# Second output projection opened five tiles wide, the last four differential heads spaced by four slots, their masks added by VectorE

## The chip, the cores and the metric

The kernel runs on one core of a Trainium2 chip. The metric is the device time of one execution in microseconds (us); a lower time is better. A time is given as the median of several runs, and one further execution is profiled; all rows of a trace come from that one.

## The reference

A two-layer decoder trunk on 256 tokens of width 2048, batch 1, in float32. Layer 0 mixes by causal pooling and a cross-attention to a memory of 256 rows; then a squared-ReLU MLP. A shared key and value projection follows. Layer 1, where the change lies, computes

```python
a = probs(q1b, k1) - lam * probs(q2b, k2)      # 12 heads, two softmax maps of width 64
o = einsum('bhqk,bkhd->bqhd', a, v)            # per head 128 wide; causal mask inside probs
token_out = rms_norm(o, subln_norm[b]) * (1.0 - lam_init)
mem_out = memory_cross_attention(...)          # 4 heads of 128, no mask
x = x + concat([token_out, mem_out]) @ w_out[1]
x = x + squared_relu_mlp(rms_norm(x, ffn_norm[1]), w_ff1[1], w_ff2[1])
```

Inside `probs` every score whose key lies behind its query gets -1e30 before the softmax. The queries stand in two blocks of 128: the first block sees 128 keys, the second 256, and in each the last 128 columns of the scores carry the triangular mask.

## The kernel before, in words

**Layout.** Activations lie transposed: 16 chunks of 128 channels by 256 tokens. Each weight is split into a high part (fp32r, a rounded float) and a low rest; a product takes the high weight against the activation's high and low halves (512 columns) and the low weight against the high half (256 columns). A block is one 128x128 weight; a group of four blocks is one 128x512 tile, loaded by SyncE, copied to the high ring by ScalarE (L158) and subtracted to the low ring by VectorE (L159). The rings have six places (`SLOTS`), and a group is prepared three groups ahead of its use (`AHEAD`).

**Slots.** `tick()` runs once each time four blocks have been used. `at(d, fn)` puts a function d slots ahead; so attention work is strewn between the matmuls of a projection. A slot in `c_tile` (L415 to L417) is four blocks with three matmuls of 256 columns each, a slot in `a_part` (L401, L403) four blocks with one matmul of 512 and one of 256 columns. The tile framework then orders each engine's instructions; engines work through their queues in that order.

**A differential head** (`diff_head`): `scores` multiplies queries and keys into two banks of tag "s" (of two), adds the mask, and has VectorE take the maxima (L1219) and ScalarE the exponentials (L1223). With `by_pe` the mask is added by TensorE, as an extra bf16 product of an identity with the mask into the same bank (L1200 to L1205: four pairs of a product and a mask product); otherwise VectorE adds it in place (L1209, L1212 the products, L1214 and L1215 the additions). Four slots later `turn` transposes the probabilities (L1238). At `pv_lag` slots, `pv` multiplies them with the values into the one bank of tag "o" (L1244 to L1246); ScalarE squares and sums (L1254), the reciprocal root follows, and VectorE scales into `osb` (L1262). With `by_pe` the bank is copied to `osb` first (L1249). `back_lag` slots on, `back` transposes the result (L1267) into its chunk of `cat1`.

**The heads' places.** The 12 heads come in three groups c of four. Heads of c = 0 and 1 start at slots 6, 10, 14, 18 after their query projection, without `by_pe`. Those of c = 2 start at 6, 8, 10, 12 with `by_pe`, their PV six slots on, their way back three more. Meanwhile four `c_tile` calls (four slots each) make the memory queries, and each memory head (`mem_head`) follows with scores (L583, one bank of "s") 4 slots after its tile, the transposition (L602) 8 and PV (L610, the bank "o") 11 after; its result is copied and subtracted into `cat1` chunks 12 to 15 (L611, L612).

**The second output projection** (`out_tiles`, call at the end of layer 1's attention). 16 output tiles, each the sum over 16 chunks of `cat1`. Three banks of tag "mm" serve the tiles. Tiles 0 to 2 are opened with a `lead` of 15 chunks in three parts, then `flush` empties the slots, then each of the three gets its last chunk `ks` = [15], and tiles 3 to 15 follow whole. A finished tile is added to the residual by two VectorE additions (L648, L649), which free its bank; then `resid_done` makes the next stage's input. The same function serves layer 0 with one lead of 13 chunks.

The MLP after it (`ffn`) takes over all banks; its first slab preparation is held back in the order until tile 2's addition (`feed.gate`).

Of the kernel before, what the change touches and what calls it, by code (L numbers as in the profile page):

```python
# [10 lines left out]
F32 = mybir.dt.float32  # L11
# [7 lines left out]
P = 128  # L19
T = 256  # L20
NK = 16
# [34 lines left out]
class Plan:  # L56
# [13 lines left out]
    def close(self):  # L70
        prep = []
        for job in self.jobs:

            late = job[0] == "S" and job[1] % 32 > 28
            if job[0] == "S" and job[2] == 0 and not late:
                prep.insert(max(0, len(prep) - KOFF), ("K", job[1]))
            if late and job[2] == 1:
                prep.append(("L", job[1]))
            prep.append(job)
        self.prep = prep  # L80
        self.where = {job: i for i, job in enumerate(prep)}
        self.loads = []
        self.need = {}
        for p in prep:
            if p[0] == "K":
                self.loads += [("S", p[1], 0), ("S", p[1], 1)]
            elif p[0] == "L":
                self.loads.append(("S", p[1], 1))
            elif p[0] == "S" and p[2] == 0 and ("S", p[1], 0) not in self.loads:
                self.loads.append(("S", p[1], 0))  # L90
            elif p[0] == "N" and p[1] % 2 == 0:
                self.loads.append(("N", p[1] // 2))
            self.need[p] = len(self.loads) - 1
        rows = sorted(self.loads, key=lambda r: r[0] == "N" and 8 * r[1] + 8 > self.npos)
        self.row = {r: h for h, r in enumerate(rows)}
        of = {}
        pos = 0
        for what in self.entries:
            of.setdefault(pos // 8, []).append(what)
            pos += what[4]  # L100
        self.order = []
        for r in rows:
            self.order += of[r[1]] if r[0] == "N" else self.slabs[r[1]][r[2]]
# [169 lines left out]
def program(ctx, tc, plan, dry, xT, memT, par, lam, cst, wst, yT):  # L273
# [5 lines left out]
    pp = ctx.enter_context(tc.tile_pool(name="pp", bufs=1, space=PSUM))  # L279
# [10 lines left out]
    def at(d, fn):  # L290
        pend.setdefault(now[0] + d, []).append(fn)

    def tick():
        now[0] += 1
        for fn in pend.pop(now[0], []):
            fn()
# [9 lines left out]
    def mmt(name):  # L306
        return pp.tile([P, 512], F32, tag="mm", bufs=3, name=name)
# [42 lines left out]
    def gcol(c):  # L350
        return param[:, c : c + 1]
# [26 lines left out]
    def split_gain(dst, src, g):  # L378
        nc.scalar.activation(dst[:, 0:T], src, AF.Copy, scale=g)
        stt(dst[:, T : 2 * T], src, g, dst[:, 0:T].bitcast(F32), ALU.mult, ALU.subtract)  # L380
# [6 lines left out]
    def a_part(ps, w, l, n, ks, xs, first=True, last=True, between=None):  # L387


        ks = list(ks)  # L390
        i = 0
        while i < len(ks):
            if between:
                between(i)
            two = []
            for k in ks[i : i + 2 - feed.pos % 2]:
                two.append((i, k % NK, *feed.block((w, l, k, n, 1))))
                feed.used()
                i += 1
            for c, k, hi, lo in two:  # L400
                nc.tensor.matmul(ps, hi, xs[:, k, :], start=first and c == 0, stop=False)  # L401
            for c, k, hi, lo in two:
                nc.tensor.matmul(  # L403
                    ps[:, T : 2 * T], lo, xs[:, k, 0:T], start=False,
                    stop=last and c == len(ks) - 1,
                )
            if feed.pos % 4 == 0:
                tick()
# [215 lines left out]
    def add_square(key, src, first, act=False):  # L624

        if first:
            acc[key] = tp.tile([P, T], F32, tag="acc", bufs=1, name="acc")
            nc.gpsimd.tensor_mul(acc[key], src, src)
            return
        sq = vt("psq")  # L630
        if act:
            nc.scalar.activation(sq, src, AF.Square)
        else:
            nc.gpsimd.tensor_mul(sq, src, src)
        nc.gpsimd.tensor_add(acc[key], acc[key], sq)
# [11 lines left out]
    def resid_add(ps, n):  # L647
        nc.vector.tensor_add(resid[:, n, :], resid[:, n, :], ps[:, 0:T])  # L648
        return nc.vector.tensor_add(resid[:, n, :], resid[:, n, :], ps[:, T : 2 * T])  # L649

    def resid_done(n, splits, square=True):
        for dst, g in splits:
            split_gain(dst[:, n, :], resid[:, n, :], gcol(g + n))
        if square:
            add_square("x", resid[:, n, :], n == 0)
# [295 lines left out]
    cat = sp.tile([P, NK, 512], F32R, tag="S0", name="cat0")  # L951
# [16 lines left out]
    ps = [mmt("mq0"), pp.tile([P, 512], F32, tag="o", bufs=1, name="mq0")]  # L968
# [14 lines left out]
    for h in range(4):  # L983
        mem_head(
            mq0[:, h, :], y0.rearrange("p (t h) -> p t h", t=2)[:, :, h], mk[:, h, :],
            lambda mb, h=h: mv[:, mb, h * P : h * P + P], ebuf[h % 2], pTb, cat[:, 12 + h, :],
# [4 lines left out]
    def group_u(g):  # L991
        up = ups[g % 2]
        for c in range(3):
            ps = mmt("u")
            a_part(ps, "w_in", 0, 3 * g + c, range(NK), xs)
            low = vt("u_c")
            nc.scalar.copy(low, ps[:, T : 2 * T])
            nc.vector.tensor_add(low, ps[:, 0:T], low)
            nc.vector.tensor_mul(up[:, c, 16:], low, x_r[0])
        w = WIN[g]  # L1000
        steps = []
        cur = up
        for i in range(g + 1):
            d = 1 << i
            lo = 2 * d - 1
            nxt = sbs[i % 2]
            steps.append((nxt[:, :, lo:], cur[:, :, lo:], cur[:, :, lo - d : 272 - d]))
            cur = nxt
        for i, (o, a, b) in enumerate(steps):
            at(i + 1, lambda o=o, a=a, b=b: nc.vector.tensor_add(o, a, b))  # L1010
        res = sbs[(g + 1) % 2][:, :, 16:]

        def mean():
            stt(res, cur[:, :, 16:], 1.0 / w, up[:, :, 16:], ALU.mult, ALU.subtract)
            inv = const[:, C_INV : C_INV + w].unsqueeze(1).to_broadcast([P, 3, w])
            nc.vector.tensor_mul(res[:, :, 0:w], cur[:, :, 16 : 16 + w], inv)
            nc.vector.tensor_sub(res[:, :, 0:w], res[:, :, 0:w], up[:, :, 16 : 16 + w])

        at(g + 2, mean)
        for c in range(3):  # L1020
            at(g + 3 + c, lambda c=c: split_plain(pooled[:, 3 * g + c, :], res[:, c, :]))
# [13 lines left out]
                    tick()  # L1035
            split_gain(cat[:, 3 * g + n, :], ps[:, 0:T], gcol(G_PS + 3 * g + n))

    def out_tiles(l, cat, lead, ks, fx, between):

        first = [mmt("wo") for _ in range(3)]  # L1040
        for i, part in enumerate(lead):
            for n in range(3):
                a_part(first[n], "w_out", l, n, part, cat, first=i == 0, last=False)
        between()
        for n in range(NK):
            if n < 3:
                ps = first[n]
                a_part(ps, "w_out", l, n, ks, cat, first=False)
            else:
                ps = mmt("wo")  # L1050
                a_part(ps, "w_out", l, n, sum(lead, []) + ks, cat)
            done = resid_add(ps, n)
            if n == 2 and not dry:
                feed.gate = done.ins.name
            resid_done(n, [(fx, G_FFN + 16 * l)])

    group_u(3)
    group_u(2)
# [9 lines left out]

    fx = sp.tile([P, NK, 512], F32R, tag="S2", name="fx0")
    lead0 = [9, 10, 11, 6, 7, 8, 3, 4, 5, 12, 13, 14, 15]  # L1070
    out_tiles(0, cat, [lead0], [0, 1, 2], fx, last_group)

    x_in = []
    down = ffn(0, fx, ("S1", "S0"), lambda n: resid_done(n, [(x_in[0], G_KV)], False))
# [40 lines left out]
    for c in range(3):  # L1115
        ps = pair_of_banks(c, "k1")
# [10 lines left out]
    for c in range(3):  # L1127
        ps = pair_of_banks(c + 1, "v1")
# [9 lines left out]
    ps = pair_of_banks(0, "mk1")  # L1138
# [4 lines left out]
    ps = pair_of_banks(1, "mv1")  # L1143
# [41 lines left out]
    cat1 = sp.tile([P, NK, 512], F32R, tag="S1", name="cat1")  # L1185
# [90 lines left out]
    for c in range(3):  # L1276
        ps = pair_of_banks(0, "q1")
        b_tile(ps, "w_in_q", 1, c, x_mx)
        rows, v = query_rows(ps, c1, 64)
        rope(rows, qtab)  # L1280
        y = query_scale(v, c1)
        for i in range(2):
            j = 2 * c + i
            q = qb[j % 3]
            at(4 + i, lambda i=i, q=q, rows=rows: turn_queries(rows, 2 * i, q))
            for g in range(2):
                h = 2 * i + g

                diff_head(
                    2 * j + g, q[g], y, *((6 + 4 * h, 8, 4 if c == 0 else 3) if c < 2 else (6 + 2 * h, 6, 3)), c == 2  # L1290
                )
    for h in range(4):
        ps = mmt("mq1")
        c_tile(ps, "w_in", 1, 12 + h, range(NK), x_mx)
        q, y = mem_query(ps[:, 0:T], mqg1, c1)
# [4 lines left out]

    fx1 = sp.tile([P, NK, 512], F32R, tag="S0", name="fx1")

    out_tiles(1, cat1, [list(range(8)), [12, 8, 9, 13], [10, 11, 14]], [15], fx1, flush)

    down = ffn(1, fx1, ("S2", "S1"), lambda n: nc.sync.dma_start(yT[:, n, :], resid[:, n, :]))
    down()
# [83 lines left out]
```

## Time and profile before

| | |
|---|---|
| median of 3 runs | 2046.35 us (2045.26 to 2046.72) |
| time of the profiled execution | 2045.64 us |
| span of its trace | 2043.9 us |
| TensorE busy (matmul) | 2037.5 us, 11060 instructions |
| VectorE busy | 1714.7 us |
| ScalarE busy | 1348.3 us |
| granted TensorE clock | 1.000 |

The span runs from the first to the last instruction; the execution's own time has 1.7 us around it. A row of the timeline gives the start in us from the span's start, the duration in us, the engine, the source line, the operation and the tiles (out<-in), the shape, and how many instructions were merged. Matmuls are pipelined, so a row's duration reaches over the starts of the next ones: what a matmul costs the engine is the distance from its start to the next start. A float32 product counts as two matmuls.

### The profile page before, as it was taken

To read this page: it belongs to the slowest core of one execution; us is meant where nothing else is said; L and a number is where in the kernel's file an instruction comes from. 1 tells how busy PE (TensorE), PEld (TensorE's weight loads), DVE (VectorE), ACT (ScalarE), POOL (GpSimd) and SP (SyncE) were. 2 spreads that over 40 slices of the span, in tenths; PEclk is the share of its full clock that TensorE was granted. 3 is DMA by queue.
4 is the path that set the end of the run, shared out by engine and by line. 5 is a ranking of instruction groups with operands and counts; after the bars stand their busy time and mean duration, and the time that the engine had idled before them with its cause. 6 is when DMAs were issued, how large, how long until landed. Compare 5 with 4: busy or idle time off the path is not lost.

```text
span 2043.9 us, 32256 instructions
## 1 busy us (share of the span) xinstructions
PE 2037.5 (100%) x11060; PEld 1753.8 (86%) x11060; DVE 1714.7 (84%) x3215; ACT 1348.3 (66%) x2505; POOL 52.4 (3%) x67
## 2 busy tenths in 40 slices
PE   9999999999999999999999999999999999999999
PEld 8888888888888888888888888888888888888888
DVE  8788889889879978999765687889879978988997
ACT  7765566667656756768665697566657666666764
POOL 0001200000000000000000000310000000000000
PEclk9999999999999999999999999999999999999999
DMA  8556556556556555655665543556555555565563
GB/s 309 180 180 193 188 171 207 198 186 208 186 197 204 187 205 191 211 169 182 192 228 189 168 141 113 187 166 207 196 195 202 189 196 196 186 207 198 195 209 134
DMA packets 110469, 390.74 MB, mean 191 GB/s; under 512 B 12256, under 2 KB 14944, under 8 KB 110304
## 3 DMA queue, kind: packets, MB, share of 16 engines
q1 hardware_dynamic: 110160, 388.59, 56.9%
q8 instruction: 86, 1.41, 0.3%
q14 instruction: 79, 0.65, 0.1%
q10 hardware_dynamic: 144, 0.10, 0.0%
HBM read 386.54 MB, written 2.10 MB: 190 GB/s over the span
## 4 chain that ended last, share of the span: by engine, by line
PE 99%; ACT 1%; DMA 0%; DVE 0%; SPq 0%; issue 0%
PE x_bank L401 33%; PE x_bank L403 16%; PE wo L401 6%; PE p L756 5%; PE p L757 5%; PE p L758 5%; PE wo L403 3%; PE u L401 2%; PE ff L401 2%; PE u L403 1%; PE k L427 1%; PE k L429 1%; PE v L427 1%; PE k L428 1%; PE v L429 1%; PE v L428 1%
## 5 line engine op out<-in xcount | busy, mean ns | idle before, releaser
L158 ACT CAST hi_ring<-raw 128x512 fp32r<-128x512 f32 x1193 | 736.2, 620 | 522.5 <-PE x_bank L401 300.2
L159 DVE TENSOR_TENSOR lo_ring<-raw,hi_ring 128x512 fp32r<-128x512 f32 x1193 | 815.9, 693 | 200.8 <-ACT hi_ring L158 157.3
L401 PE MATMUL x_bank<-fx,hi_ring 128*128 128x512 f32 x1920 | 601.8, 395 | 0.0
L403 PEld LDWEIGHTS x_bank<-fx,lo_ring 128*128 128x128 f32 x1920 | 360.6, 188 | 84.0
L403 PE MATMUL x_bank<-fx,lo_ring 128*128 128x256 f32 x1920 | 377.2, 278 | 0.0
L401 PEld LDWEIGHTS x_bank<-fx,hi_ring 128*128 128x128 f32 x1920 | 301.2, 189 | 9.4
L401 PE MATMUL x_bank<-z,hi_ring 128*128 128x512 f32 x960 | 301.0, 395 | 0.0
L159 DVE TENSOR_TENSOR lo_ring<-slab,hi_ring 128x1024 fp32r<-128x1024 f32 x188 | 229.9, 1223 | 54.2 <-ACT hi_ring L158 53.4
L158 ACT CAST hi_ring<-slab 128x1024 fp32r<-128x1024 f32 x188 | 196.8, 1047 | 72.9 <-PE x_bank L401 37.5
L403 PEld LDWEIGHTS x_bank<-z,lo_ring 128*128 128x128 f32 x960 | 180.3, 188 | 41.9
L403 PE MATMUL x_bank<-z,lo_ring 128*128 128x256 f32 x960 | 188.6, 278 | 0.0
L401 PE MATMUL wo<-cat,hi_ring 128*128 128x512 f32 x512 | 163.2, 399 | 1.4 <-DVE resid L649 0.8
L401 PEld LDWEIGHTS x_bank<-z,hi_ring 128*128 128x128 f32 x960 | 151.8, 189 | 6.5 <-ACT room L682 0.4
L403 PEld LDWEIGHTS wo<-cat,lo_ring 128*128 128x128 f32 x512 | 95.9, 188 | 21.9
L682 ACT COPY room<-x_bank 128x512 f32<-128x512 f32 x180 | 104.8, 582 | 2.0 <-PE x_bank L403 2.0
L403 PE MATMUL wo<-cat,lo_ring 128*128 128x256 f32 x512 | 101.5, 278 | 0.0
L756 PE MATMUL p<-hi_ring,sit 128*128 128x512 f32 x256 | 100.4, 392 | 0.0
L757 PE MATMUL p<-hi_ring,sit 128*128 128x512 f32 x256 | 100.1, 391 | 0.0
L758 PE MATMUL p<-lo_ring,sit 128*128 128x512 f32 x256 | 99.6, 389 | 0.0
L727 ACT ACTIVATE room<-room 128x256 f32<-128x256 f32 x128 | 53.2, 416 | 45.5 <-DVE room L310 45.3
L401 PEld LDWEIGHTS wo<-cat,hi_ring 128*128 128x128 f32 x512 | 78.8, 189 | 3.1 <-PE wo L403 1.3
L756 PE MATMUL p<-hi_ring,z 128*128 128x512 f32 x192 | 75.1, 391 | 0.0
(313 smaller groups left out, 3099.0 us busy)
## 6 DMA issues: line engine op xcount, KB each, us to landing
raw<-in_w SPq DMA_DIRECT2D x595, 512.0 KB, 3.8
slab<-in_w SPq DMA_DIRECT2D x124, 512.0 KB, 3.5
resid<-in_x SPq DMA_DIRECT2D x8, 256.0 KB, 5.3
room<-in_w SPq DMA_DIRECT2D x4, 512.0 KB, 4.2
memraw<-in_mem SPq DMA_DIRECT2D x4, 512.0 KB, 4.1
out_y<-resid SPq DMA_DIRECT2D x16, 128.0 KB, 1.8
memraw<-in_mem SPq DMA_DIRECT2D x7, 256.0 KB, 6.4
raw<-in_w SPq DMA_DIRECT2D x3, 256.0 KB, 3.7
```

What stands on the lines that cost most here:

```text
L158: self.nc.scalar.copy(hi, src)
L159: self.nc.vector.tensor_sub(lo, src, hi.bitcast(F32))
L401: nc.tensor.matmul(ps, hi, xs[:, k, :], start=first and c == 0, stop=False)
L403: nc.tensor.matmul(ps[:, T : 2 * T], lo, xs[:, k, 0:T], start=False, stop=last and c == len(ks) - 1,)
L427: nc.tensor.matmul(ps[t], xl, hi, start=k == 0, stop=False)
L428: nc.tensor.matmul(ps[t], xh, hi, start=False, stop=False)
L429: nc.tensor.matmul(ps[t], xh, lo, start=False, stop=k == NK - 1)
L682: nc.scalar.copy(x, ps)
L727: at(3, lambda: nc.scalar.activation(stage[i % 8], y[:, 0:T], AF.Square))
L756: nc.tensor.matmul(ps, a[1], hi, start=first, stop=False)
L757: nc.tensor.matmul(ps, a[0], hi, start=False, stop=False)
L758: nc.tensor.matmul(ps, a[0], lo, start=False, stop=last)
```

## The change

Three parts, all in layer 1. First, the last four heads start at slots 6, 10, 14, 18 instead of 6, 8, 10, 12, with PV seven slots on instead of six, and without `by_pe`: VectorE adds their masks, and the copy of the bank "o" (L1249) goes for them, so that the bank is read until the scaling. Second, `out_tiles` opens five tiles: 0 to 2 with 11 chunks in two parts, then 3 and 4 with the same 11 chunks, these two in banks of tag "s"; after the flush each of the five gets the last five chunks 9, 14, 10, 15, 11, and tiles 5 to 15 follow whole in the three "mm" banks. Third, the additions to the residual (`close`) of tiles 1 to 4 are put 1, 3, 7 and 10 slots later. Layer 0 keeps its order.

```diff
-    def out_tiles(l, cat, lead, ks, fx, between):
-        first = [mmt("wo") for _ in range(3)]
-        for i, part in enumerate(lead):
-            for n in range(3):
-                a_part(first[n], "w_out", l, n, part, cat, first=i == 0, last=False)
-        between()
-        for n in range(NK):
-            if n < 3:
-                ps = first[n]
-                a_part(ps, "w_out", l, n, ks, cat, first=False)
-            else:
-                ps = mmt("wo")
-                a_part(ps, "w_out", l, n, sum(lead, []) + ks, cat)
+    def out_tiles(l, cat, lead, ks, fx, between, later):
+        def tile_bank(n):
+            if n in (3, 4):
+                return pp.tile([P, 512], F32, tag="s", bufs=2, name="wo")
+            return mmt("wo")
+
+        def close(ps, n):
             done = resid_add(ps, n)
             if n == 2 and not dry:
                 feed.gate = done.ins.name
             resid_done(n, [(fx, G_FFN + 16 * l)])
+
+        first = []
+        for tiles, parts in lead:
+            for part in parts:
+                for n in tiles:
+                    if n == len(first):
+                        first.append(tile_bank(n))
+                    a_part(
+                        first[n], "w_out", l, n, part, cat, first=part is parts[0], last=False
+                    )
+        between()
+        every = sum(lead[0][1], [])
+        for n in range(NK):
+            if n < len(first):
+                ps = first[n]
+                a_part(ps, "w_out", l, n, ks, cat, first=False)
+            else:
+                ps = tile_bank(n)
+                a_part(ps, "w_out", l, n, every + ks, cat)
+            if n < len(later) and later[n]:
+                at(later[n], lambda ps=ps, n=n: close(ps, n))
+            else:
+                close(ps, n)
...
-    out_tiles(0, cat, [lead0], [0, 1, 2], fx, last_group)
+    out_tiles(0, cat, [(range(3), [lead0])], [0, 1, 2], fx, last_group, ())
...
-                    2 * j + g, q[g], y, *((6 + 4 * h, 8, 4 if c == 0 else 3) if c < 2 else (6 + 2 * h, 6, 3)), c == 2
+                    2 * j + g, q[g], y, 6 + 4 * h, *((8, 4 if c == 0 else 3) if c < 2 else (7, 3)), False
...
-    out_tiles(1, cat1, [list(range(8)), [12, 8, 9, 13], [10, 11, 14]], [15], fx1, flush)
+    parts = [list(range(8)), [12, 8, 13]]
+    lead1 = [(range(3), parts), (range(3, 5), [parts[0] + parts[1]])]
+    out_tiles(1, cat1, lead1, [9, 14, 10, 15, 11], fx1, flush, (0, 1, 3, 7, 10))
```

## Prediction

> **What bounds the kernel now.** I read the page first, then the sums by stretches, TensorE's waits, and the timeline around the change. On the page I look at the engines' shares and at the chain that ended last.
>
> ```profile
> PE 2037.5 (100%) x11060; PEld 1753.8 (86%) x11060; DVE 1714.7 (84%) x3215; ACT 1348.3 (66%) x2505; POOL 52.4 (3%) x67
> PE 99%; ACT 1%; DMA 0%; DVE 0%; SPq 0%; issue 0%
> ```
>
> TensorE works the whole span and is 99% of the chain. So a change gains only what it takes out of TensorE's queue or out of TensorE's idle time. The sums by stretches (busy us and count for each engine) show how little idle time there is where the change lies:
>
> ```profile
> 1200.00:1250.00 50.00, 49.95 (x375) 46.56 (x374) 42.34 (x154) 43.76 (x145) 0.00 (x0) 1.00 0.40 127
> 1250.00:1280.00 30.00, 28.84 (x172) 24.68 (x172) 22.66 (x71) 19.88 (x57) 2.07 (x3) 1.00 0.42 141
> ```
>
> The last four heads start at 1220 and the first output tiles close at 1275. TensorE (first busy column) lacks 0.05 us in the first stretch and 1.16 us in the second. TensorE's waits from 1250 to 1400 name all of the latter:
>
> ```profile
> PE wo L401 <- DVE resid L649: 0.6, 1, 0.6
> PE wo L401 <- DVE cat L612: 0.6, 1, 0.6
> ```
>
> These are the two things that can go: the mask products and two waits at the closing of tiles 0 to 3.
>
> **Part 1: the masks.** One head with masks by TensorE, then one with masks by VectorE, each from its first product to the next projection matmul:
>
> ```profile
> 1225.75 0.60 PE L1200 MATMUL s<-big,att 128*128 128x256 f32 x2
> 1226.18 0.22 PE L1201 MATMUL s<-mkb,idb 128*128 128x128 bf16 x1
> 1226.24 0.65 PE L1200 MATMUL s<-big,att 128*128 128x256 f32 x2
> ...
> 1227.39 0.22 PE L1205 MATMUL s<-mkb,idb 128*128 128x128 bf16 x1
> 1227.42 0.36 PE L415 MATMUL mq<-x_mx,hi_ring 128*128 128x256 f32 x1
> 1227.62 0.28 PE L416 MATMUL mq<-x_mx,hi_ring 128*128 128x256 f32 x1
> 1227.74 0.28 PE L417 MATMUL mq<-x_mx,lo_ring 128*128 128x256 f32 x1
> ```
> ```profile
> 1211.03 1.03 PE L1209 MATMUL s<-big,att 128*128 128x256 f32 x4
> 1211.90 0.61 PE L1212 MATMUL s<-big,att 128*128 128x128 f32 x4
> 1212.26 0.36 PE L415 MATMUL mq<-x_mx,hi_ring 128*128 128x256 f32 x1
> ```
>
> From start to start the first takes 1227.42 - 1225.75 = 1.67 us, the second 1212.26 - 1211.03 = 1.23 us. The difference is 0.44 us a head, four heads: **-1.76 us**. It holds more than the 16 mask matmuls themselves: the distance from the first mask to the next product is 0.06 us, and the product behind it is longer too (0.65 against 0.60). The Trainium skill (TensorE: Matmul & The Clock Gate, section "Wait — 56ns, not 53.3ns?") gives 55.6 ns from start to start for warm bf16 matmuls of 128 columns. The 0.06 us agrees; by that figure alone 16 masks would give an estimate of -0.89 us and the sum would end 0.87 us higher, but the page's figure leaves out what the neighbours lose, and the row decides.
>
> What VectorE takes on, from the groups by shape between 1200 and 1280:
>
> ```profile
> L1214 DVE TENSOR_TENSOR s<-s,const 128x256 f32<-128x256 f32 x2 | 0.9, 428 | 0.2 <-PE s L1209 0.2
> L1249 DVE COPY osb<-do 128x256 f32<-128x256 f32 x4 | 1.7, 420 | 0.3
> L1262 DVE TENSOR_SCALAR osb<-do,o_y 128x128 f32<-128x128 f32 x8 | 2.4, 344 | 0.1
> L1262 DVE TENSOR_SCALAR osb<-osb,o_y 128x128 f32<-128x128 f32 x8 | 1.9, 282 | 0.0
> ```
>
> Eight additions of 0.43 us, less four copies of 0.42, and eight scalings out of the bank at 0.344 instead of 0.282: 3.4 - 1.7 + 0.5 = +2.2 us. VectorE is idle for 7.66 us in the first stretch above and for 7.34 in the second, and its low-ring work is three groups ahead of TensorE. I cost it at nothing; without that cover it is +2.2 us. Behind a mask addition, which waits for the scores, stand ring subtractions on the same queue; those already stand so behind the heads of c = 1, whose additions waited 0.2 us (the row's last number) without a TensorE wait.
>
> **Part 2: the spacing.** Four heads over 12 slots instead of 6 add no instruction. In the built order TensorE leaves the projection for attention work 31 times from just ahead of the first memory-query tile to the end of the output projection, against 29 before; inside the output projection it is 14 against 11. Each return costs a longer first pair. A pair after an interruption, and a quiet one:
>
> ```profile
> 1261.92 0.82 PE L401 MATMUL wo<-cat,hi_ring 128*128 128x512 f32 x2
> 1262.58 0.40 PE L403 MATMUL wo<-cat,lo_ring 128*128 128x256 f32 x2
> ...
> 1278.60 0.62 PE L401 MATMUL wo<-cat,hi_ring 128*128 128x512 f32 x2
> 1279.06 0.40 PE L403 MATMUL wo<-cat,lo_ring 128*128 128x256 f32 x2
> ```
>
> The two high products take 0.66 us against 0.46: 0.20 us. In the memory tile above it is 1227.62 - 1227.42 = 0.20 against 0.12: 0.08 us. Three more of one and one fewer of the other: at most 0.6 - 0.08 = 0.5, at least three of 0.08 less one: 0.16. I take **+0.3 us**, between them.
>
> **Part 3: the closing.** The two waits with their surroundings:
>
> ```profile
> 1275.06 0.28 PE L403 MATMUL wo<-cat,lo_ring 128*128 128x256 f32 x1
> 1275.91 0.50 PE L401 MATMUL wo<-cat,hi_ring 128*128 128x512 f32 x1 [0.57 <-DVE cat L612]
> 1276.25 0.28 PE L403 MATMUL wo<-cat,lo_ring 128*128 128x256 f32 x1
> 1276.36 0.40 PE L401 MATMUL wo<-cat,hi_ring 128*128 128x512 f32 x1
> ...
> 1276.96 0.28 PE L403 MATMUL wo<-cat,lo_ring 128*128 128x256 f32 x1
> 1277.83 0.71 PE L401 MATMUL wo<-cat,hi_ring 128*128 128x512 f32 x2 [0.59 <-DVE resid L649]
> 1278.37 0.39 PE L403 MATMUL wo<-cat,lo_ring 128*128 128x256 f32 x2
> ```
>
> A 256-column matmul costs 0.11 to 0.12 (1276.25 to 1276.36). Here the next start comes 0.85 and 0.87 us later: 0.73 + 0.75. The first products after the gaps cost 0.34 instead of 0.23 and 0.54 instead of 0.46: 0.1 and 0.08. Together **-1.66 us** if both waits go.
>
> They do by count. In the built order, 48 of the 55 opening blocks stand before the last memory PV is done, so 7 blocks and the chunks 9, 14, 10 of tile 0 stand between it and chunk 15: 10 blocks of 0.35 us (0.70 us a pair from 1278.60) are 3.5 us, against 0.73 us that are missing now. Tile 5 needs tile 0's bank only 20 blocks (7 us) after tile 0's last product, against 0.75 us missing now. What would be late next is the last head's chunk 11, the fifth to be closed: its transposition follows the last PV directly, 11 blocks, 3.8 us ahead. The later additions of tiles 1 to 4 lie beside tiles 5 to 15 (11 x 16 blocks of 0.35, 61 us). The memory stays as it is: one slab load stands two places later in SyncE's queue, and the preparation that `feed.gate` holds back moves on with tile 2. I cost these at nothing.
>
> **A new wait.** Without the copy the bank "o" is held until the scaling. Its hold, from the start of PV to the end of the scaling or of the copy, is in three heads (the first two without, the third with the copy):
>
> ```profile
> 1201.67 0.38 PE L1244 MATMUL do<-big,att 128*128 128x128 f32 x2
> 1205.59 0.60 DVE L1262 TENSOR_SCALAR osb<-do,o_y 128x128 f32<-128x128 f32 x2
> ```
> ```profile
> 1230.57 0.39 PE L1244 MATMUL do<-big,att 128*128 128x128 f32 x2
> 1237.83 0.61 DVE L1262 TENSOR_SCALAR osb<-do,o_y 128x128 f32<-128x128 f32 x2
> ```
> ```profile
> 1238.52 0.47 PE L1244 MATMUL do<-big,att 128*128 128x128 f32 x2
> 1239.47 0.42 DVE L1249 COPY osb<-do 128x256 f32<-128x256 f32 x1
> ```
>
> That is 4.5, 7.9 and 1.4 us. The next user of the bank is a memory PV. In the built order TensorE has about 8.6, 8.8, 7.3 and 3.6 us of its own work between the two for the four heads (the last: a PV of 0.7 and 8.3 projection blocks of 0.35). Only the last is short: a hold of 4.5 us stalls it by 0.9, one of 7.9 by 4.3 and the third by 0.6 more. VectorE does mask and maximum work inside the 4.5 us, and the last head has no head behind it, so the hold should be nearer to 4. I take **+0.5 us**, bounds 0 and 4.9. TensorE stands in order, so all projection blocks wait behind that PV.
>
> **Sum.** -1.76 + 0.3 - 1.66 + 0.5 = -2.62 us. The profiled execution took 2045.64 us (1.7 around its span), so its counterpart would take 2043.0; the median is 0.7 higher, 2046.35, and I forecast the median: **2043.7 us**, by -0.13%.
>
> **Rivals.**
> - *The bank "o" is held long (slower).* Price 4.9 instead of 0.5: 2048.1 us. It beats the gain from a last hold of 3.6 + 2.6 + 0.5 = 6.7 us on. For it: the 7.9 us row, in a heavily loaded stretch. Against it: few other heads are left then. The Trainium skill (PSUM — Partial Sum Buffer, section "Summary: rules for kernel authors") says to evacuate promptly, which speaks against dropping the copy. By that rule this rival holds; the 1.4 us row agrees that the copy frees the bank early. Chance 0.13.
> - *VectorE becomes the bound.* All of its +2.2 us falls on TensorE: 2045.9 us. For it: 42.34 of 50 us busy and a strict order. Against: no TensorE wait on a ring there now. Chance 0.11.
> - *A larger gain.* Each mask matmul is worth its busy 0.22 us (16 x 0.22 = 3.5), no new wait and no price for the returns: 2046.35 - 3.5 - 1.66 = 2041.2 us. Chance 0.07.
> - *The closing waits stay*, because something other than the counted chunks holds them: 2045.4 us. Chance 0.03.
>
> **How the numbers follow.** The forecast has 0.66. Its terms reach from 2043.1 (0.16 for the returns, no new wait) to 2044.3 (0.5 and 0.9), and the runs before lie 1.1 below to 0.4 above their median: 2042.0 to 2044.7. The range 2042.0 to 2047.0 takes in the VectorE case and the returning waits and leaves out most of the first rival and of the larger gain. Differences under 0.2%, 4.1 us, are about what a measurement of this kernel cannot tell from none. Below 2042.26 lie the larger gain and the forecast's edge: 0.12. Above 2050.44 lies only a hold of about 9 us in all four heads: 0.06. Between: 0.82.
>
> **What would show it.** In the profile after: no L1201 or L1205; scores of the last heads at 1.23 us; no wait of a wo matmul on L612 or L649; VectorE's busy time up by about 2 us; at most one wait of about 0.5 us at the last memory PV (L610) or the transposition next to it. Several waits on L1262, or on the low ring, would make the forecast wrong.

## The result and the profile after

| | before | after |
|---|---|---|
| median of 18 runs each | 2045.70 us (2045.12 to 2046.72) | 2042.14 us (2041.53 to 2042.47) |
| profiled execution | 2045.64 us | 2042.28 us |
| span of its trace | 2043.9 us | 2040.5 us |

The ratio is 0.9982, with a 95% interval of 0.9976 to 0.9988: 3.56 us faster. The forecast of 2043.7 us is 1.6 us above it. In a second series the changed kernel stood at 2042.09 against 2045.65 us, 3.56 us apart again.

The page of the changed kernel, busy time of each engine and the shares of the chain that ended last:

```profile
span 2040.5 us, 32228 instructions
PE 2035.0 (100%) x11044; PEld 1752.8 (86%) x11044; DVE 1715.7 (84%) x3219; ACT 1348.9 (66%) x2505; POOL 53.3 (3%) x67
...
PE 98%; ACT 1%; DVE 0%; DMA 0%; SPq 0%; issue 0%
```

TensorE has 16 instructions fewer, the masks, and still works the whole span. VectorE has 4 more, eight additions less four copies. The same two stretches as before (length, then busy us and count of TensorE, its weight loads, VectorE, ScalarE, GpSimd, then clock, DMA share, GB/s):

```profile
1200.00:1250.00 50.00, 49.95 (x370) 47.27 (x369) 43.94 (x157) 43.70 (x140) 0.00 (x0) 1.00 0.42 138
1250.00:1280.00 30.00, 29.88 (x177) 25.81 (x176) 22.58 (x68) 19.86 (x61) 0.00 (x0) 1.00 0.39 133
```

The idle 1.16 us of TensorE in the second stretch have become 0.12. TensorE's wait list from 1200 to 1400 us is empty, where that of before named two waits. The scores of the last head, and what comes next on TensorE (rows of the timeline, TensorE alone):

```profile
1251.26 1.03 PE L1228 MATMUL s<-big,att 128*128 128x256 f32 x4
1252.13 0.50 PE L563 MATMUL st_mq<-ones_h,mq_sq 128*128 128x2 f32 x4
...
1253.03 0.61 PE L1231 MATMUL s<-big,att 128*128 128x128 f32 x4
1253.40 0.48 PE L403 MATMUL wo<-cat,lo_ring 128*128 128x256 f32 x2
```

0.87 and 0.37 us from start to start make 1.24 us (L1228 and L1231 are L1209 and L1212 moved down by 19 lines). The first closing blocks, where the kernel before stopped for 0.73 and 0.75 us:

```profile
1276.56 0.40 PE L403 MATMUL wo<-cat,lo_ring 128*128 128x256 f32 x2
1276.79 0.40 PE L401 MATMUL wo<-cat,hi_ring 128*128 128x512 f32 x1
1277.03 0.28 PE L403 MATMUL wo<-cat,lo_ring 128*128 128x256 f32 x1
1277.14 0.40 PE L401 MATMUL wo<-cat,hi_ring 128*128 128x512 f32 x1
1277.38 0.28 PE L403 MATMUL wo<-cat,lo_ring 128*128 128x256 f32 x1
```

Starts follow each other by 0.24 and 0.11 us with no gap.

**A finer measure.** The interval of a ratio reaches about 1.8 us to each side in the experiments, as wide as a term of the sum. So I also measure the **stage** in each trace: from the first matmul of the memory queries (L415), which stands ahead of all that the change moves on TensorE, to the first matmul of the MLP (L401 on `fx`). For before and after (each row's first number is the start):

```profile
1206.95 0.28 PE L415 MATMUL mq<-x_mx,hi_ring 128*128 128x256 f32 x1
...
1350.35 0.40 PE L401 MATMUL ff<-fx,hi_ring 128*128 128x512 f32 x1
```
```profile
1206.81 0.28 PE L415 MATMUL mq<-x_mx,hi_ring 128*128 128x256 f32 x1
...
1347.16 0.40 PE L401 MATMUL ff<-fx,hi_ring 128*128 128x512 f32 x1
```

143.40 us have become 140.35: **-3.05 us in the stage**. The trace of the second series gives 1347.02 - 1206.66 = 140.36. Only the changed kernel was traced twice, so this repeat is known for it alone.

**Outside the stage: layer 0.** `out_tiles` serves layer 0 too, and its new `tile_bank` gives tiles 3 and 4 banks of tag "s" there as well. TensorE's list of waits over the whole span of before has this line, and one of its two waits is in layer 0's output projection, where tile 3 needs the bank of tile 0:

```profile
PE wo L401 <- DVE resid L649: 0.8, 2, 0.6
```
```profile
181.67 0.39 PE L403 MATMUL wo<-cat,lo_ring 128*128 128x256 f32 x2
182.29 0.70 PE L401 MATMUL wo<-cat,hi_ring 128*128 128x512 f32 x2 [0.23 <-DVE resid L649]
182.84 0.39 PE L403 MATMUL wo<-cat,lo_ring 128*128 128x256 f32 x2
```

The same three rows after the change:

```profile
182.10 0.39 PE L403 MATMUL wo<-cat,lo_ring 128*128 128x256 f32 x2
182.33 0.62 PE L401 MATMUL wo<-cat,hi_ring 128*128 128x512 f32 x2
182.79 0.40 PE L403 MATMUL wo<-cat,lo_ring 128*128 128x256 f32 x2
```

They span 1.17 us before and 0.69 after. From the last matmul of the pooling (L1032) to the 40th matmul behind it, the five traces with the old `out_tiles` take 7.53 to 7.55 us and the eight with the new one 7.06 to 7.09: **-0.47 us**, which neither the description of the change nor the prediction has. With the stage that is -3.52 us, against 3.56 between the medians.

Where the stage begins varies from 1206.35 to 1208.30 us over all traces: by this half microsecond, and for the rest by what happens in the first 10 us of an execution. That is why lengths, not ends, are compared.

### The profile page after: what moved, and what is told of

Same layout as the page of the kernel before. It is cut to its first block, busy times and chain, and to the rows that moved or that the text cites. A ratio compares the mean times of both kernels' runs of the same rounds, so it can differ in the third digit from the quotient of the medians.

```text
span 2040.5 us, 32228 instructions
## 1 busy us (share of the span) xinstructions
PE 2035.0 (100%) x11044; PEld 1752.8 (86%) x11044; DVE 1715.7 (84%) x3219; ACT 1348.9 (66%) x2505; POOL 53.3 (3%) x67
## 4 chain that ended last, share of the span: by engine, by line
PE 98%; ACT 1%; DVE 0%; DMA 0%; SPq 0%; issue 0%
PE x_bank L401 33%; PE x_bank L403 16%; PE wo L401 6%; PE p L756 5%; PE p L757 5%; PE p L758 5%; PE wo L403 3%; PE u L401 2%; PE ff L401 2%; PE u L403 1%; PE k L427 1%; PE v L429 1%; PE k L429 1%; PE k L428 1%; PE v L427 1%; PE v L428 1%
## 5 line engine op out<-in xcount | busy, mean ns | idle before, releaser
L401 PE MATMUL x_bank<-fx,hi_ring 128*128 128x512 f32 x1920 | 601.8, 395 | 0.0
L401 PEld LDWEIGHTS x_bank<-fx,hi_ring 128*128 128x128 f32 x1920 | 301.3, 189 | 9.4
L401 PE MATMUL x_bank<-z,hi_ring 128*128 128x512 f32 x960 | 300.9, 395 | 0.0
L401 PE MATMUL wo<-cat,hi_ring 128*128 128x512 f32 x512 | 162.6, 397 | 0.0
L401 PEld LDWEIGHTS x_bank<-z,hi_ring 128*128 128x128 f32 x960 | 151.8, 189 | 6.4 <-ACT room L682 0.4
L401 PEld LDWEIGHTS wo<-cat,hi_ring 128*128 128x128 f32 x512 | 78.9, 189 | 1.0 <-DVE cat L310 0.4
```

## The experiments

The theory: the three parts add up, and what the missing copy costs is the hold of the bank "o". The rivals: the gain lies in the closing alone; the spacing or the later additions carry it; TensorE's masks are dearer than the rows say. All stages side by side, in the order of their length:

| kernel | stage us | against before | median us, before in that series | ratio (95%) |
|---|---|---|---|---|
| e7 masks twice | 144.73 | +1.33 | 2047.10, 2045.58 | 1.0007 (0.9998 to 1.0016) |
| e4 three tiles opened | 144.08 | +0.68 | 2046.26, 2045.70 | 1.0003 (0.9994 to 1.0011) |
| before | 143.40 | | | |
| e1 masks alone | 143.10 | -0.30 | 2045.27, 2045.70 | 0.9998 (0.9989 to 1.0007) |
| e3 closing alone | 141.72 | -1.68 | 2043.83, 2045.70 | 0.9992 (0.9983 to 1.0001) |
| e8 masks, with copy | 141.67 | -1.73 | 2044.41, 2045.58 | 0.9992 (0.9983 to 1.0001) |
| e2 masks back on TensorE | 140.88 | -2.52 | 2042.41, 2045.70 | 0.9983 (0.9975 to 0.9992) |
| e10 copy in all heads | 140.40 | -3.00 | 2042.15, 2045.65 | 0.9983 (0.9974 to 0.9992) |
| after, second series | 140.36 | -3.04 | 2042.09, 2045.65 | 0.9982 (0.9973 to 0.9991) |
| e5 no later additions | 140.35 | -3.05 | 2041.95, 2045.58 | 0.9981 (0.9973 to 0.9990) |
| e9 old places, with copy | 139.97 | -3.43 | 2042.17, 2045.65 | 0.9984 (0.9975 to 0.9993) |
| e6 copy kept | 139.72 | -3.68 | 2041.24, 2045.58 | 0.9978 (0.9969 to 0.9987) |

The stage leaves out layer 0; the medians of e2, e3, e5, e6, e9, e10 and of the changed kernel hold its 0.47 us too.

**e3, the closing alone.** The changed kernel's `out_tiles` and its call, with the heads of before.

```diff
-                    2 * j + g, q[g], y, 6 + 4 * h, *((8, 4 if c == 0 else 3) if c < 2 else (7, 3)), False
+                    2 * j + g, q[g], y, *((6 + 4 * h, 8, 4 if c == 0 else 3) if c < 2 else (6 + 2 * h, 6, 3)), c == 2
```

> The kernel before with the new output projection alone (five tiles opened, last five chunks 9, 14, 10, 15, 11, later additions); the heads stand as before, with masks by TensorE. Theory A (the two closing waits are worth 1.5 to 1.66 us, and nothing else changes): -1.5 to -1.7 against before, no wait of a wo matmul on L612 or L649. Rival (the closing waits only hide other work; they come back as waits on a ring or a bank): 0 to -0.5.

```profile
1206.46 0.28 PE L415 MATMUL mq<-x_mx,hi_ring 128*128 128x256 f32 x1
...
1348.18 0.40 PE L401 MATMUL ff<-fx,hi_ring 128*128 128x512 f32 x1
```

-1.68 us, and both closing waits are gone from the list. The closing by itself is worth what its two gaps were.

**e5, no later additions.** The changed kernel, each tile closed at once.

```diff
-    out_tiles(1, cat1, lead1, [9, 14, 10, 15, 11], fx1, flush, (0, 1, 3, 7, 10))
+    out_tiles(1, cat1, lead1, [9, 14, 10, 15, 11], fx1, flush, ())
```

> The changed kernel with the additions of tiles 1 to 4 at once instead of 1, 3, 7 and 10 slots later. Theory A (they lie beside 61 us of projection, and tile 5 needs tile 0's bank 7 us later): no change against the changed kernel, within 0.3 us, no wait of a wo matmul. Rival (five additions and splits in a row make VectorE late for the low ring just there): +0.5 to +1.5 us.

The stage is that of the changed kernel to 0.01 us (1346.79 - 1206.44). The third part of the change does nothing here.

**e4, three tiles opened.** The kernel before with the new heads; three tiles get 14 chunks, and then 15 and 11.

```diff
-                    2 * j + g, q[g], y, *((6 + 4 * h, 8, 4 if c == 0 else 3) if c < 2 else (6 + 2 * h, 6, 3)), c == 2
+                    2 * j + g, q[g], y, 6 + 4 * h, *((8, 4 if c == 0 else 3) if c < 2 else (7, 3)), False
-    out_tiles(1, cat1, [list(range(8)), [12, 8, 9, 13], [10, 11, 14]], [15], fx1, flush)
+    out_tiles(1, cat1, [list(range(8)), [12, 8, 9, 13], [10, 14]], [15, 11], fx1, flush)
```

> The new heads (four slots apart, masks by VectorE) with the old way of closing: three tiles opened, with 14 chunks in 42 blocks, chunks 15 and 11 last, additions at once. Theory A (the five tiles are what hides the later end of the heads): the masks give -1.8, but the last PV and the last way back stand right at the closing, and the two closing waits grow from 1.5 to 3 to 5 us in all: 0 to +2 against before. Rival (the order of the chunks is enough, five tiles are not needed): -3 against before, no closing wait.

TensorE's waits in this kernel from 1200 to 1400 us (total, times, longest):

```profile
PE do L1244 <- DVE cat L612: 0.8, 1, 0.8
PE wo L401 <- DVE cat L612: 0.8, 1, 0.8
PE wo L401 <- DVE resid L649: 0.7, 1, 0.7
PE o_t L1267 <- DVE osb L1262: 0.4, 2, 0.2
```

The closing waits are back, and a PV of a head now waits for the memory head before it. The stage is 3.73 us longer than with five tiles (144.08 against 140.35). So the heads four slots apart need the new closing: the rival that the order of the chunks is enough (-3) is out. The run goes back to three open tiles and also keeps two chunks for last instead of five, and does not say which of the two matters more.

**e1, the masks alone.** The kernel before; VectorE adds the masks of the last heads, which stay at their places. The copy, tied to `by_pe`, goes with it.

```diff
-                    2 * j + g, q[g], y, *((6 + 4 * h, 8, 4 if c == 0 else 3) if c < 2 else (6 + 2 * h, 6, 3)), c == 2
+                    2 * j + g, q[g], y, *((6 + 4 * h, 8, 4 if c == 0 else 3) if c < 2 else (6 + 2 * h, 6, 3)), False
```

> The kernel before with one part of the change alone: the last four heads get their masks from VectorE (no mask products, no copy of the bank o), at their old places two slots apart, old output projection. Theory A (each head gives TensorE 0.44 us back, the bank o costs nothing because the order is built around its hold): -1.8 us against the kernel before, 2043.9. Theory B (the bank o held 7 to 9 us stalls TensorE when heads stand two slots, about 5 us, apart): 2 to 4 us a head later, +6 to +14 us, waits on L1262 in TensorE's list.

Its waits from 1200 to 1400 us, then the ends of its stage:

```profile
PE do L1244 <- DVE osb L1262: 0.6, 1, 0.6
PE wo L401 <- DVE resid L649: 0.6, 1, 0.6
PE wo L401 <- DVE cat L612: 0.6, 1, 0.6
```
```profile
1207.37 0.28 PE L415 MATMUL mq<-x_mx,hi_ring 128*128 128x256 f32 x1
...
1350.47 0.40 PE L401 MATMUL ff<-fx,hi_ring 128*128 128x512 f32 x1
```

Only -0.30 us instead of the masks' 1.76, and far from the +6 to +14 of theory B: neither held. A PV waits for a scaling, which reads the bank "o": the mechanism of the first rival, in a place without the spacing.

**e8, the same with the copy kept.** Put to find out whether the bank takes the rest.

```diff
-            if by_pe:
+            if h >= 8:
                 nc.vector.tensor_copy(osb, o)
                 o = osb
```

> The kernel before with masks of the last four heads by VectorE at the old places, as in the first run, but with the copy of the bank o kept. Theory C (what kept the first run from -1.7 us was the bank o held until the scaling): -1.5 to -1.8 against before, no wait on L1262. Rival (it was the two slots between heads and VectorE's queue, copy or not): -0.3 to -0.6 as in the first run.

```profile
1208.30 0.28 PE L415 MATMUL mq<-x_mx,hi_ring 128*128 128x256 f32 x1
...
1349.97 0.40 PE L401 MATMUL ff<-fx,hi_ring 128*128 128x512 f32 x1
```

-1.73 us: with the copy the masks bring the full amount, and in e1 the bank took 1.43 us of it, of which 0.6 is the listed wait. (Its median is 1.2 us below that of before; its profiled execution, the slowest of its runs with 2045.41 us, began the stage 1.35 us later than that of before.)

**e6, the changed kernel with the copy.** The same edit in the changed kernel.

> The changed kernel with the copy of the bank o kept for the last four heads (VectorE still adds the masks). Theory C, formed from the four runs before: with VectorE's masks the bank o is held about 8 us and TensorE loses 0.07 to 0.2 us at each PV and way back, about 1.1 us in all, too short to be listed as waits; with the copy they go. Stage from the first memory query tile to the MLP 139.2 to 139.6 us against 140.36, time -0.8 to -1.1 against the changed kernel, about 2041.2. Rival (the small losses belong to the interruptions themselves, or VectorE's four more copies cost as much): no change, within 0.3 us, or slower.

```profile
1206.51 0.28 PE L415 MATMUL mq<-x_mx,hi_ring 128*128 128x256 f32 x1
...
1346.23 0.40 PE L401 MATMUL ff<-fx,hi_ring 128*128 128x512 f32 x1
```

0.63 us less than the changed kernel in the stage, a little short of what was expected (139.2 to 139.6 us); in the median 0.9 less than the changed kernel in the first series, and 0.7 less than e5, which ran beside it. This is the fastest kernel of the study: 2041.24 us, 4.34 below before. The profile lists no wait that went away, so the places must be read from the starts. In the changed kernel, VectorE's last scaling and TensorE around the last memory PV (L610):

```profile
1272.66 0.61 DVE L1281 TENSOR_SCALAR osb<-do,o_y 128x128 f32<-128x128 f32 x2
```
```profile
1273.01 0.28 PE L403 MATMUL wo<-cat,lo_ring 128*128 128x256 f32 x1
1273.41 1.10 PE L610 MATMUL mo<-att,mv 128*128 128x256 f32 x4
1274.16 0.47 PE L403 MATMUL wo<-cat,lo_ring 128*128 128x256 f32 x1
```

And with the copy:

```profile
1268.71 0.42 DVE L1268 COPY osb<-do 128x256 f32<-128x256 f32 x1
```
```profile
1271.06 0.40 PE L403 MATMUL wo<-cat,lo_ring 128*128 128x256 f32 x2
1271.29 1.03 PE L610 MATMUL mo<-att,mv 128*128 128x256 f32 x4
1271.97 0.82 PE L401 MATMUL wo<-cat,hi_ring 128*128 128x512 f32 x2
```

In the first the scaling ends at 1273.27 and the memory PV starts at 1273.41, 0.40 us after a matmul that costs 0.11 to 0.12 elsewhere: 0.28 us late, and the PV itself takes 0.75 instead of 0.68. In the second the bank was free 2.16 us before the PV started. One more place of this kind in the changed kernel adds 0.10: the memory PV at 1246.35 starts 0.06 us after a scaling has ended and takes 0.96 instead of 0.86 us. That makes 0.45 us seen where a scaling has just freed the bank. Two heads' PVs are late by 0.07 and 0.11 us as well (1260.07 and 1269.68), but they follow the memory head's own subtraction (L612, which ends at 1259.98 and 1269.62) and not a scaling. The two built orders differ in other places too: the 0.63 is the measurement, and its places are known only in part.

**e2, the masks back on TensorE.** The changed kernel with `by_pe` for the last heads, copy included.

```diff
-                    2 * j + g, q[g], y, 6 + 4 * h, *((8, 4 if c == 0 else 3) if c < 2 else (7, 3)), False
+                    2 * j + g, q[g], y, 6 + 4 * h, *((8, 4 if c == 0 else 3) if c < 2 else (7, 3)), c == 2
```

> The changed kernel with one part undone: the masks of the last four heads are added by TensorE again, and the bank o is copied again; spacing and closing stay. Theory A (0.44 us a head by the distance to the next projection matmul): +1.8 us against the changed kernel, that is -1.8 against the kernel before. Rival (a mask product costs only its own 0.056 us, 16 x 0.056 = 0.9, and the rest of the gain is from the spacing): -2.7 against before. Rival (the gain has nothing to do with the masks): -3.5 against before.

```profile
1206.35 0.28 PE L415 MATMUL mq<-x_mx,hi_ring 128*128 128x256 f32 x1
...
1347.23 0.40 PE L401 MATMUL ff<-fx,hi_ring 128*128 128x512 f32 x1
```

0.53 us more than the changed kernel, but that weighs the masks against the copy. Against e3 (TensorE's masks at the old places) the spacing alone is worth 140.88 - 141.72 = -0.84 us. Against e6, which has the copy too, the masks are worth 139.72 - 140.88 = -1.16 us at the new places. By its number, -2.52 us against before, this run is nearest to the rival that prices a mask at its own 0.056 us. Added up from start to start over the stage, though, e2 has 0.87 us more than e6 in the mask products and 0.85 more in the score products beside them, 1.72 us as in the theory; the rest of its stage is 0.56 us shorter.

**e9, the old places.** The changed kernel with the copy, its last heads back at 6, 8, 10, 12 and PV after six slots.

```diff
-                    2 * j + g, q[g], y, 6 + 4 * h, *((8, 4 if c == 0 else 3) if c < 2 else (7, 3)), False
+                    2 * j + g, q[g], y, *((6 + 4 * h, 8, 4 if c == 0 else 3) if c < 2 else (6 + 2 * h, 6, 3)), False
```

> The kernel before with the new output projection, masks of the last four heads by VectorE and the copy of the bank o kept, but the heads at their old places two slots apart: all of the change but the spacing, and the copy. If the parts add up (closing -1.68, masks with copy -1.73 in the stage from the first memory query tile to the MLP): stage 140.0, 0.3 us longer than with the new places and the copy (139.72), time about -3.4 against before. Rival (the places are worth 0.8 us of their own, as the run with TensorE's masks at the new places read): stage 140.5 or more. Rival (with the copy the old places are as good or better): 139.7 or less.

```profile
1207.43 0.28 PE L415 MATMUL mq<-x_mx,hi_ring 128*128 128x256 f32 x1
...
1347.40 0.40 PE L401 MATMUL ff<-fx,hi_ring 128*128 128x512 f32 x1
```

-3.43 us against before, which is the closing and the masks added up (-1.68 - 1.73 = -3.41). With VectorE's masks the spacing is worth 139.72 - 139.97 = -0.25 us, less than with TensorE's.

**e7, each mask twice.** The kernel before with every mask product issued twice: the mask is added twice.

```diff
                     nc.tensor.matmul(s1[:, m, :], q[:, m, P:T], kk, start=True, stop=False)
+                    nc.tensor.matmul(s1[:, m, P:T], idb, mkb, start=False, stop=False)
                     nc.tensor.matmul(s1[:, m, P:T], idb, mkb, start=False, stop=True)
...
                     nc.tensor.matmul(s0[:, m, :], q[:, m, 0:P], kk, start=True, stop=False)
+                    nc.tensor.matmul(s0[:, m, :], idb, mkb, start=False, stop=False)
                     nc.tensor.matmul(s0[:, m, :], idb, mkb, start=False, stop=True)
```

> The kernel before with each of the 16 mask products of the last four heads issued twice in a row (the mask is added twice). Price of a mask product by itself: if it is its own distance of 0.055 us, the stage grows by 16 x 0.055 = 0.9 us, and the rest of the 0.105 us a mask is what the change from float32 to bf16 and back costs the neighbour. If the whole 0.105 us belongs to each mask: +1.7 us. If masks hide beside other work: 0.

```profile
1221.32 0.22 PE L1201 MATMUL s<-mkb,idb 128*128 128x128 bf16 x1
1221.38 0.22 PE L1202 MATMUL s<-mkb,idb 128*128 128x128 bf16 x1
1221.43 0.65 PE L1200 MATMUL s<-big,att 128*128 128x256 f32 x2
```

The stage grew by 1.33 us, 0.083 us for each added mask: between the two expectations. Of this, 1.20 us stand at the mask products: from start to start the second mask costs 0.05 to 0.06 us, and at one place, 1222.34, a transposition that waits for ScalarE (L1175) starts 0.36 us after a mask. Without this one wait, 0.30 us, the growth is about 1.0 us, near the first expectation. Taking all 16 away was worth 1.73 us, 0.108 each (e8). The dearer-masks rival (0.22 us each) is out.

**e10, the copy in all heads.** If the copy is worth 0.63 us in four heads, does it help in the others?

```diff
-            if by_pe:
+            if True:
                 nc.vector.tensor_copy(osb, o)
                 o = osb
```

> The changed kernel with the copy of the bank o for all 12 heads, not only the last four. Theory C (every hold of the bank costs TensorE slivers of 0.07 to 0.2 us): -0.1 to -0.5 us more than the kernel with the copy in four heads, most of it before the first memory query tile and at the first PV after it; about 2041.0. Rival (VectorE is the tighter engine in the query projection, eight more copies of 0.42 us make it late): no gain or +0.3 to +1.

It does not: the stage is 140.40 us, 0.68 more than with the copy in the last four (e6). Added up from start to start, the heads' PVs take 0.70 us more than in e6 and the memory scores 0.54 more, the memory queries 0.54 less, and in this built order memory scores stand between the products of two PVs (at 1236.95 and 1248.06). That speaks for the order rather than for a late VectorE, but no run here tells the two apart.

**The changed kernel once more**, beside e9 and e10.

> The changed kernel unaltered, beside the two others of this call. Expected -3.5 us against the kernel before, stage 140.36, that is 0.6 to 0.9 us above the kernel with the copy kept in four heads.

140.36 us of stage and the same 3.56 us of difference in the medians: the stage repeats to 0.01 us.

## Why the prediction was nearly right

Its sum was -2.62 us; the stage shows -3.05, and layer 0 another -0.47. The median of 2042.14 us lies only 0.14 us inside the lower end of the range, in the part below 2042.26 to which the prediction gave a chance of 0.12. Term by term, with the runs that measure each:

| term | predicted | measured | from |
|---|---|---|---|
| closing | -1.66 | -1.68 | e3 - before |
| masks | -1.76 | -1.73 | e8 - before |
| spacing ("returns") | +0.3 | -0.25 | e6 - e9 |
| bank "o" without copy | +0.5 | +0.63 | after - e6 |
| sum in the stage | -2.62 | -3.03 | |
| layer 0, tile 3's wait | not in the sum | -0.47 | 5 traces against 8 |

- **What bounds.** Right: TensorE's queue and its idle time were all there was to gain. The sum left out one idle time: the wait in layer 0. The description of the change says "Layer 0 keeps its order"; the order stayed, but the banks of two tiles did not.
- **Closing.** Right to 0.02 us, mechanism included: the two waits went, nothing else came late. The count of blocks ahead of chunk 15 held: 48 of the 55 stand before the last memory PV, and chunk 15 is first used at 1278.20, where its subtraction ended at 1275.76. e4 shows the other side of it. The later additions, costed at nothing, cost nothing (e5).
- **Masks.** Right at the old places, as far as the bank is copied. The quiet row of a head of c = 1 gave the price (1.23 us a head; 1.24 in the trace after). The Trainium skill (TensorE: Matmul & The Clock Gate, section "Wait — 56ns, not 53.3ns?") gives 55.6 ns for a warm bf16 matmul of this size, an estimate of 0.89 us for all. The starts in e7 agree with 55.6 ns, and so do the 0.84 us from start to start that e8 saves in mask products. But e8 saves another 0.66 us in the score products beside them: what the mask's neighbours lose has to be counted with it, as the prediction did.
- **VectorE.** Its cover held. Its busy time rose by 1.0 us over the span and by 1.6 - 0.1 = 1.5 in the two stretches, where 2.2 were reckoned, and no TensorE wait on a low ring appeared. The rival of VectorE as the bound did not occur.
- **Spacing: the step that failed.** "Each return costs a longer first pair", three more returns, +0.3 us. The longer first pair is in the rows, but the count of returns in a whole built order does not price the spacing. In the pairs of runs that differ in the places alone, TensorE leaves the projection, counted as in the prediction, 27 times instead of 30 with TensorE's masks (e2 against e3) and 33 times instead of 32 with VectorE's (e6 against e9); the stage falls both times, by 0.84 and by 0.25 us. e6, with the most returns of all, has the shortest stage. That the two amounts differ also means that masks and spacing are not quite separate: together they bring 139.72 - 141.72 = -2.00 us (e6 - e3), which splits into -1.75 and -0.25 if the masks go first, and into -0.84 and -1.16 if the spacing goes first. From start to start, e2 is shorter than e3 by 0.53 us in the low-ring products of the output projection, by 0.38 in the heads' PVs and by 0.32 in the memory scores, and longer by 0.26 in the memory transpositions. So the gain is spread over the stage; why this order has it stays open.
- **Bank "o".** The place was right and the working too simple; that the size came near is in part luck. One wait of 0.5 us was forecast "at the last memory PV"; there the trace has 0.28 + 0.07 us, 0.10 stand at the first memory PV, and the rest of the 0.63 is not placed. The forecast counted the last hold at about 4 us; it is 1273.27 - 1269.68 = 3.59. But the hold of the first of the four heads, from its PV to the end of its scaling, is 8.6 us:

```profile
1237.71 0.38 PE L1263 MATMUL do<-big,att 128*128 128x128 f32 x2
```
```profile
1245.68 0.61 DVE L1281 TENSOR_SCALAR osb<-do,o_y 128x128 f32<-128x128 f32 x2
```
```profile
1246.35 1.12 PE L610 MATMUL mo<-att,mv 128*128 128x256 f32 x4
```

  The heads after it hold the bank 8.8 and 7.5 us, so for three of four the 7.9 us row was the nearer one. What saved the time is the place of the next user: the memory PV stands in TensorE's queue where the bank has just come free (1246.29 to 1246.35), and TensorE has projection blocks until then. The first rival's bound of 4.9 us was therefore far off here, but its mechanism is real: with the old places it took 1.43 us (e1 against e8). The Trainium skill (PSUM — Partial Sum Buffer, section "Summary: rules for kernel authors") says to evacuate promptly, and gives the small size of the memory as the reason. The runs agree with the advice for these four heads, where the copy of 0.42 us on VectorE is worth 0.63 us of TensorE's time. For the other eight they do not (e10).

Of the 1.56 us between 2043.7 and 2042.14 us, 0.65 are there because the median of before is 2045.70 over 18 runs and was 2046.35 over three; 0.43 are the terms of the stage, and 0.47 the wait in layer 0.

## What to carry to other kernels

Price a removed instruction by the distance between starts with and without it, neighbours included, and a gap at the end of a stage by what it lacks; both held here to 0.03 us with the heads at their old places. Do not price a new order by counting its interruptions. When a function serves two places, look for its waits at both: two more banks for the output tiles took 0.47 us out of a layer that was thought unchanged. Dropping a copy that frees a bank early is not free even when no wait is listed afterwards: compare the bank's hold with the start of its next user, and try the copy again after moving the work around it.

## What the runs showed that was not expected

- A stall can be spread so thin that the wait list stays empty: without the copy the changed kernel loses 0.63 us, of which 0.45 are found in pieces of 0.07 to 0.28 us from start to start, and TensorE shows as busy for 49.95 of 50 us around one of them.
- A bf16 product of 128 columns between float32 products starts the next matmul after 0.06 us, and yet was worth 0.108 us when 16 of them were removed: 0.84 us went in the masks and 0.66 in the float32 products beside them.
- The stage of one kernel repeats to 0.01 us (140.35 and 140.36), while the starts of all traces lie up to 1.95 us apart, of which 0.47 is layer 0 and the rest arises in the first 10 us.
